# State-space mixer: order of the decay rows' loads, the sums of squares, the last output products and the norm

## The chip, the cores and the metric

The kernel runs on one core of a Trainium2 chip. A core has TensorE (matrix products; PE in the profile), VectorE (DVE), ScalarE (ACT), GpSimd (POOL) and SyncE (SP), which work beside one another, each through its own list of instructions in order, and wait for one another by semaphores. Data comes by DMAs that an engine's queue issues; here the weights come by SyncE's queue and the decay rows by ScalarE's. The metric is the device time of one launch in microseconds, the median of several runs.

## What is computed

A trunk of two layers over 512 tokens and 1024 features, in float32: an attention layer and a state-space layer, each followed by a convolutional feed-forward block and layer norms. The change lies in the second layer's mixer and the norm behind it, in the reference:

```python
def step(state, inp):                       # one chunk of 128 tokens
    xk, dtk, bk, ck = inp
    la = jnp.cumsum(dtk * a_g, axis=1)
    seg = la[:, :, None] - la[:, None, :]
    decay = jnp.exp(jnp.where(causal, seg, -jnp.inf))
    xdt = xk * dtk[..., None]
    cb = jnp.einsum('bign,bjgn->bijg', ck, bk)
    y = jnp.einsum('bijgh,bjghp->bighp', cb[..., None] * decay, xdt)
    y = y + jnp.einsum('bign,bghpn->bighp', ck, state) * jnp.exp(la)[..., None]
    ...                                     # state of the next chunk
y = y + d_skip[:, None] * xs
y = y.reshape(B, S, SSD_INNER) * jax.nn.silu(z)
y = group_rms_norm(y, norm_w)               # over the 512 features of a head group
return y @ w_out
...
x = layer_norm(DEEPNORM_ALPHA * x + m, ln_mix_g[i], ln_mix_b[i])
```

## The kernel before

Every large product is made in three passes (`mm3`, L105, L106, L107: high by high, high by low, low by high part of the operands). So each operand is split first: `split` copies the high part on ScalarE (L73) and subtracts it on VectorE (L76). Weights go through the same split, or, where a gain is folded in, through L98 and L99.

The mixer `ssd()` goes through four head groups g, and in each through four chunks c of 128 tokens. `Inputs(g).part(0..3)` makes a group's inputs: the projections and convolutions of B and C, of x, and of z (`acc<-xTh,w`, z on L1006 and L1007). While group g is scanned, the parts of group g+1 stand between its chunks and fill TensorE; so do the output products of group g-1 (`mixer_out`, `run_out`, `acc<-w,yT`), in the first two chunks. In the last group there are no further inputs.

`Scan.weights(c)` (L885) prepares the decays of a chunk: a DMA of 512 KB (L890, tile `lab`, also called E) puts the rows of the running sums into one of three buffers, TensorE makes cb (L893), ScalarE applies eight ReLUs (L897) and one exponential (L898), VectorE multiplies by cb (L899), GpSimd makes xdt (L901). `Scan.chunk(c)` (L911) loads el by two smaller DMAs (L922), makes the state product (L927), `intra` and `inter` (both L908), sums y on VectorE (L941 to L943), calls `weights(c + 1)`, multiplies by z (L948) and splits the result into `yT` (L73, L76). One yT tile holds two chunks. Then come the squares on ScalarE (L953), their sum over four blocks on VectorE (L955), the product `ss` with a column of ones on TensorE (L957) and the inverse root (L126 on VectorE, a power on GpSimd, L127), whose result `rsg` scales the output products where `run_out` adds them to the residual x (L861, VectorE).

After the last group `mixer_last` goes through the token tiles t = 0 to 3: output products of the group for both halves of the features, statistics (L179), then `Norm.finish`. Its ordinary form makes two passes on VectorE (L196, L197); its shared form, which the attention layer uses, scales on ScalarE (L192), multiplies on VectorE (L193) and adds on GpSimd (L194). `xT_of` then transposes x on TensorE (L136, tile `xTb`) and splits it for the feed-forward block.

The instructions are not in the order of the code: a scheduler places them on each engine by a planned timeline, within what buffers and operands allow. `acc` banks of PSUM are four, in two pairs; ss, cb, intra, inter and xTb take turns in four others.

## Time and profile before

| what | value |
|---|---|
| median of 3 runs | 1482.93 us (1482.7 to 1485.36) |
| profiled execution, time | 1487.44 us |
| its span | 1485.7 us, mean granted clock 0.992 |
| busy: TensorE, VectorE, ScalarE, GpSimd | 98%, 57%, 44%, 10% |

The span is what the profile covers of one execution; busy shares are of the span. The granted clock is that of TensorE, as a share of its full speed. A wait is idle time of an engine, put down to what ended last before it went on. The scan of the mixer reaches from about 745 to 1048 us, the norm behind it to about 1073.

### The profile page before, as it was taken

Reading aid. Unit: us, or ns where it says so; the run is one execution under the profiler, and the core shown is the slowest. Engines: PE = TensorE matmul, PEld = TensorE weight load, DVE = VectorE, ACT = ScalarE, POOL = GpSimd, SP = SyncE. Lnnn points to the kernel's source line nnn. Section 1 sums busy time; section 2 is a strip of 40 time slices with the busy share of each in tenths; the row PEclk is TensorE's granted clock in tenths of the full one; section 3 lists DMA queues with packets and bytes.
Section 4 is the critical chain, followed back from the end, with each engine's and each line's share of the span. In section 5 each row is a group of like instructions: output and inputs, shape, how many; then the busy total and the mean of one; then the engine's idle time right before and its main releaser. Section 6 shows DMA issues by size and latency. Waiting matters only on the chain.

```text
span 1485.7 us, 19157 instructions
## 1 busy us (share of the span) xinstructions
PE 1456.1 (98%) x7264; PEld 1199.8 (81%) x7264; DVE 851.5 (57%) x1465; ACT 658.7 (44%) x1261; POOL 142.1 (10%) x245
## 2 busy tenths in 40 slices
PE   9998999999999999999998999999799999999998
PEld 7875878888888888889876787887688888888887
DVE  5366786554545333846685867777854544433382
ACT  5476663443443222444765555453243443422331
POOL 2134313000000000000121101121100000000000
PEclk9999999999999999999999999999899999999999
DMA  6304142332333324423433332432232332333411
GB/s 232 110 29 153 58 146 72 100 98 88 99 99 100 99 86 164 139 69 117 118 121 100 107 122 90 128 118 95 87 100 99 93 98 93 100 100 93 162 57 57
DMA packets 51931, 155.92 MB, mean 105 GB/s; under 512 B 6400, under 2 KB 13312, under 8 KB 51840
## 3 DMA queue, kind: packets, MB, share of 16 engines
q1 hardware_dynamic: 39168, 135.49, 28.7%
q10 hardware_dynamic: 12672, 19.21, 4.1%
q8 instruction: 57, 0.93, 0.3%
q14 instruction: 34, 0.28, 0.1%
HBM read 148.26 MB, written 5.37 MB: 103 GB/s over the span
## 4 chain that ended last, share of the span: by engine, by line
PE 94%; DVE 3%; ACT 1%; DMA 1%; issue 1%; POOL 0%; ACTq 0%; DVEq 0%; POOLq 0%
PE acc L105 25%; PE acc L107 25%; PE acc L106 25%; PE pg L105 2%; PE pg L106 2%; PE pg L107 2%; PE s L329 1%; PE intra L908 1%; PE xTb L136 1%; PE pt L356 1%; PE o L368 1%; PE state L927 1%; PE inter L908 1%; DVE w L76 1%; PE om L105 1%
## 5 line engine op out<-in xcount | busy, mean ns | idle before, releaser
L76 DVE TENSOR_TENSOR w<-raw,w 128x512 fp32r<-128x512 f32 (+1 forms) x438 | 300.5, 695 | 288.5 <-ACT w L73 288.2
L73 ACT ACTIVATE w<-raw 128x512 fp32r<-128x512 f32 (+1 forms) x438 | 268.8, 625 | 422.5 <-PE acc L107 364.6
L106 PE MATMUL acc<-xTl,w 128*128 128x512 f32 (+1 forms) x1104 | 414.4, 376 | 0.5 <-DVE xTl L76 0.5
L105 PE MATMUL acc<-xTh,w 128*128 128x512 f32 (+1 forms) x1104 | 414.4, 377 | 0.0
L107 PE MATMUL acc<-xTh,w 128*128 128x512 f32 (+1 forms) x1104 | 414.0, 375 | 0.0
L106 PEld LDWEIGHTS acc<-xTl,w 128*128 128x128 f32 x1104 | 208.2, 189 | 37.8 <-issue 1.0
L107 PEld LDWEIGHTS acc<-xTh,w 128*128 128x128 f32 x1104 | 208.2, 189 | 37.6 <-issue 0.9
L105 PEld LDWEIGHTS acc<-xTh,w 128*128 128x128 f32 x1104 | 207.7, 189 | 37.7 <-DVE z L1007 0.5
L106 PE MATMUL acc<-w,h 128*128 128x512 f32 x352 | 137.1, 390 | 0.0
L107 PE MATMUL acc<-w,h 128*128 128x512 f32 x352 | 136.8, 390 | 0.0
L105 PE MATMUL acc<-w,h 128*128 128x512 f32 x352 | 136.7, 389 | 0.0
L604 DVE SCALAR_TENSOR_TENSOR conv<-acc,cw,conv 128x511 f32<-128x511 f32 x88 | 65.6, 746 | 87.7 <-ACT conv L602 87.7
L127 POOL TENSOR_TENSOR mv<-rs,half_neg 128x1 f32<-128x1 f32 x16 | 13.0, 815 | 754.8 <-DVE rs L126 754.8
L106 PEld LDWEIGHTS acc<-w,h 128*128 128x128 f32 x352 | 66.1, 188 | 13.7
L107 PEld LDWEIGHTS acc<-w,h 128*128 128x128 f32 x352 | 66.1, 188 | 13.6
L105 PEld LDWEIGHTS acc<-w,h 128*128 128x128 f32 x352 | 66.1, 188 | 13.6
L602 ACT ACTIVATE conv<-acc,cw 128x512 f32<-128x512 f32 x44 | 34.3, 780 | 84.1 <-PE acc L107 84.1
L628 DVE TENSOR_TENSOR conv<-conv,acc 128x512 f32<-128x512 f32 x44 | 30.2, 687 | 60.1 <-PE acc L107 57.6
L105 PE MATMUL acc<-w,yT 128*128 128x512 f32 x128 | 52.9, 413 | 3.8 <-ACT yT L73 3.8
L604 DVE SCALAR_TENSOR_TENSOR cv<-acc,scw,cv 128x511 f32<-128x511 f32 (+2 forms) x72 | 52.0, 740 | 6.0 <-ACT cv L602 5.7
L107 PE MATMUL acc<-w,yT 128*128 128x512 f32 x128 | 52.2, 410 | 0.6 <-DVE yT L76 0.6
L106 PE MATMUL acc<-w,yT 128*128 128x512 f32 x128 | 51.9, 405 | 0.0
(278 smaller groups left out, 2053.5 us busy)
## 6 DMA issues: line engine op xcount, KB each, us to landing
raw<-in_w_up SPq DMA_DIRECT2D x88, 512.0 KB, 3.5
raw<-in_w_down SPq DMA_DIRECT2D x44, 512.0 KB, 3.5
raw<-in_w_xbc SPq DMA_DIRECT2D x24, 512.0 KB, 3.6
raw<-in_w_ple_gate SPq DMA_DIRECT2D x16, 512.0 KB, 4.6
raw<-in_w_z SPq DMA_DIRECT2D x16, 512.0 KB, 3.5
lab<-rows ACTq DMA_DIRECT2D x16, 512.0 KB, 4.2
raw<-in_w_sout SPq DMA_DIRECT2D x16, 512.0 KB, 3.5
raw<-in_w_qkv SPq DMA_DIRECT2D x11, 512.0 KB, 4.6
```

The lines of the kernel that those rows point to most:

```text
L73: A.activation(h, src, AF.Copy)
L76: eng.tensor_tensor(l, src, h.bitcast(F32), op=OP.subtract)
L105: T.matmul(ps, lh, rh, start=start, stop=False)
L106: T.matmul(ps, lh, rl, start=False, stop=False)
L107: T.matmul(ps, ll, rh, start=False, stop=stop)
L136: T.transpose(b[:, k * P:(k + 1) * P], src[:, (half * 4 + k) * P:(half * 4 + k + 1) * P], ident)
L329: T.matmul(b[:, :e], q[:, ts], k[:, :e], start=n == 0, stop=n == len(qk) - 1)
L356: T.transpose(b[:, at:at + P], self.soft[x][2][i][:, t], ident)
L602: A.activation(f, ps, AF.Identity, bias=cw[:, taps:taps + 1], scale=cw[:, taps - 1:taps])
L604: V.scalar_tensor_tensor(f[:, k:], ps[:, :S - k], cw[:, taps - 1 - k:taps - k], f[:, k:], op0=OP.mult, op1=OP.add)
L628: V.tensor_tensor(g, g, pu, op=OP.mult)
L908: T.matmul(b[64 * x:64 * x + 64, k * P:(k + 1) * P], weights[:, h * 64:h * 64 + 64], moving(h), start=True, stop=True)
```

## The change

The decay rows and el of a chunk are fetched by a function of its own, `fetch(n)`, which `weights` calls for the following chunk, and which is called once for the first chunk ahead of all inputs. The sum over four blocks of squares is made by two additions in place of a reduction. The product ss and the inverse root leave `chunk` for `norm(c)`, which is called after the filling products of the chunk. In the last group, the output products of token tiles 0 and 1 are called within chunks 2 and 3 (`out_last`), ahead of these chunks' `norm`; those of tiles 2 and 3 stay behind the scan. And the norm behind the mixer takes its shared form.

```diff
-            def mixer_last(sc, w, ln, new, t):
-                for half in range(2):
-                    run_out(sc, w[half], half, t)
-                    ln.stats(t, xs[t], half)
-                ln.finish(t, xs[t], new)
+            ahead = {}
+
+            def fetch(n):
+
+                if n < 4 * NT:
+                    c = n % NT
+                    hs = slice(c * 32 + n // NT * 8, c * 32 + n // NT * 8 + 8)
+                    lab, el = three.tile([P, 8, P], F32, tag="lab", name="lab"), None
+                    nc.scalar.dma_start(lab.rearrange("p h i -> p (h i)"),
+                                        rows[hs, :].rearrange("h i -> (h i)").partition_broadcast(P))
+                    if c:
+                        el = two.tile([P, 4, P], F32, tag="el", name="el")
+                        for x in range(2):
+                            src = erows[hs, :].rearrange("(k x) i -> x k i", x=2)[x]
+                            nc.scalar.dma_start(el[64 * x:64 * x + 64], src.partition_broadcast(64))
+                    ahead[n] = lab, el

...
-                    E = three.tile([P, 8, P], F32, tag="lab", name="lab")
-                    nc.scalar.dma_start(E.rearrange("p h i -> p (h i)"),
-                                        rows[hs, :].rearrange("h i -> (h i)").partition_broadcast(P))
+                    E, el = ahead.pop(4 * g + c)
+                    fetch(4 * g + c + 1)
...
-                    self.E, self.xdt = E, xdt
+                    self.E, self.el, self.xdt = E, el, xdt
...
-                    E, xdt = self.E, self.xdt
+                    E, el, xdt = self.E, self.el, self.xdt
                     half, xd = c % 2, self.xd[c // 2]
                     hc = slice(half * P, (half + 1) * P)
-                    if c:
-                        el = two.tile([P, 4, P], F32, tag="el", name="el")
-                        for x in range(2):
-                            src = erows[hs, :].rearrange("(k x) i -> x k i", x=2)[x]
-                            nc.scalar.dma_start(el[64 * x:64 * x + 64], src.partition_broadcast(64))
...
                     sq = scr("sq").rearrange("p (k i) -> p k i", i=P)
                     A.activation(sq, y, AF.Square)
-                    s1 = st.tile([P, P], F32, tag="s1", name="s1", bufs=2)
-                    V.tensor_reduce(s1, sq.rearrange("p k i -> p i k"), axis=mybir.AxisListType.X, op=OP.add)
+                    V.tensor_tensor(sq[:, :2], sq[:, :2], sq[:, 2:], op=OP.add)
+                    self.sq = st.tile([P, P], F32, tag="s1", name="s1", bufs=2)
+                    V.tensor_tensor(self.sq, sq[:, 0], sq[:, 1], op=OP.add)
+
+                def norm(self, c):
                     b = bank("ss")
-                    T.matmul(b[:, :1], s1, ones[:, :1], start=True, stop=True)
+                    T.matmul(b[:, :1], self.sq, ones[:, :1], start=True, stop=True)

                     rsqrt(self.rs[:, c:c + 1], b[:, :1], 1.0 / 512, 4 * RMS_EPS)
...
+            fetch(0)
             ins = Inputs(0)
             for i in range(4):
                 ins.part(i)
             prev = None
+            last = {}
+
+            def out_last(half, t):
+                if t == 0:
+                    last[half] = load_out(3, half)
+                run_out(sc, last[half], half, t)
+
             for g in range(4):
                 sc = Scan(ins)
                 ins = Inputs(g + 1) if g < 3 else None
@@ -1020,12 +1036,19 @@
                         ins.part(c)
                     if prev and c < 2:
                         mixer_out(prev, c)
+                    elif not ins:
+                        for half in range(2):
+                            out_last(half, c - 2)
+                    sc.norm(c)
                 prev = sc
...
             ln = Norm(three, "ln_mix", 1, ("lab", "lab"))
             new = new_xT()
-            w = [load_out(3, half) for half in range(2)]
             for t in range(NT):
-                mixer_last(sc, w, ln, new, t)
+                for half in range(2):
+                    if t > 1:
+                        out_last(half, t)
+                    ln.stats(t, xs[t], half)
+                ln.finish(t, xs[t], new, True)
```

In the changed kernel the lines lie further down: the fetch's DMAs are L876 (lab) and L882 (el), ReLU and exponential L907 and L908, cb L903, the pairs of intra and inter L918, y L946 to L953, the squares L958, the two additions L959 and L961, ss L965, z L1014 and L1015.

ScalarE, end of group 0, where the decays of the next group's first chunk are prepared; raw and w are weights, y and z the tiles named above. Before:

```order
L890 DMA lab_7136<-rows_5715 128x1024
L922 DMA el_7342<-erows_5716 64x4x128
L897 ACTIVATE lab_7136<-lab_7136,la_5703 128x128 x8
L73 ACTIVATE w_7172<-raw_7170 128x512
L922 DMA el_7342<-erows_5716 64x4x128
L73 ACTIVATE yT_6584<-y_6699 128x4x128
L953 ACTIVATE sq_6724<-y_6699 128x512
L1006 ACTIVATE z_6733<-acc_6742 128x512
...
L73 ACTIVATE w_7175<-raw_7170 128x512
L898 ACTIVATE lab_7136<-lab_7136 128x1024
```

After:

```order
L876 DMA lab_6922<-rows_5715 128x1024
L73 ACTIVATE w_7184<-raw_7179 128x512
L907 ACTIVATE lab_6922<-lab_6922,la_5703 128x128 x8
L882 DMA el_6924<-erows_5716 64x4x128 x2
L908 ACTIVATE lab_6922<-lab_6922 128x1024
L73 ACTIVATE yT_6591<-y_6704 128x4x128
L958 ACTIVATE sq_6729<-y_6704 128x512
L1014 ACTIVATE z_6734<-acc_6743 128x512
```

The DMA stands where it stood, with the eight ReLUs behind it; a weight split is ahead of the ReLUs, and the exponential, which stood behind the z, is ahead of the split of y.

TensorE, last group, behind inter of chunk 2, from cb on: `yT_8547` is the tile of chunks 0 and 1. Before (31 products on that tile follow cb, the first 11 are shown):

```order
L893 MATMUL cb_8799<-CT_7685,BT_7684 128x128
L107 MATMUL acc_8919<-w_8892,yT_8547 128x512
L105 MATMUL acc_8919<-w_8897,yT_8547 128x512
L106 MATMUL acc_8919<-w_8897,yT_8547 128x512
L107 MATMUL acc_8919<-w_8897,yT_8547 128x512
L105 MATMUL acc_8919<-w_8900,yT_8547 128x512
L106 MATMUL acc_8919<-w_8900,yT_8547 128x512
L107 MATMUL acc_8919<-w_8900,yT_8547 128x512
L105 MATMUL acc_8959<-w_8873,yT_8547 128x512
L106 MATMUL acc_8959<-w_8873,yT_8547 128x512
L107 MATMUL acc_8959<-w_8873,yT_8547 128x512
L105 MATMUL acc_8959<-w_8876,yT_8547 128x512
```

After (`yT_8567` is that of chunks 0 and 1, `yT_8833` that of chunks 2 and 3):

```order
L903 MATMUL cb_8816<-CT_7695,BT_7694 128x128
L106 MATMUL acc_8950<-w_8876,yT_8567 128x512
L107 MATMUL acc_8950<-w_8876,yT_8567 128x512
L105 MATMUL acc_8950<-w_8881,yT_8567 128x512
L106 MATMUL acc_8950<-w_8881,yT_8567 128x512
L107 MATMUL acc_8950<-w_8881,yT_8567 128x512
L105 MATMUL acc_8950<-w_8884,yT_8567 128x512
L106 MATMUL acc_8950<-w_8884,yT_8567 128x512
L107 MATMUL acc_8950<-w_8884,yT_8567 128x512
L105 MATMUL acc_9037<-w_8843,yT_8833 128x512
L106 MATMUL acc_9037<-w_8843,yT_8833 128x512
```

Of the 31 products eight are left there; the others stand ahead of chunk 2's ss, and the ninth row behind cb reads chunk 2's yT.

TensorE, last group, at chunk 3, from ss to the first product that reads chunk 3's part of the yT tile (`acc_9071` before, `acc_9096` after). Before:

```order
L957 MATMUL ss_8823<-ones_5706,s1_8821 128x1
L908 MATMUL intra_8832<-lab_8797,xdt_8813 64x128 x8
L908 MATMUL inter_8841<-CT_7685,state_8772 64x128 x8
L107 MATMUL acc_9031<-w_8897,yT_8816 128x512
L105 MATMUL acc_9031<-w_8900,yT_8816 128x512
L106 MATMUL acc_9031<-w_8900,yT_8816 128x512
L107 MATMUL acc_9031<-w_8900,yT_8816 128x512
L105 MATMUL acc_9071<-w_8873,yT_8816 128x512
```

After:

```order
L965 MATMUL ss_8901<-ones_5706,s1_8839 128x1
L918 MATMUL intra_8907<-lab_8681,xdt_8830 64x128 x8
L918 MATMUL inter_8916<-CT_7695,state_8791 64x128 x8
L105 MATMUL acc_9096<-w_8843,yT_8833 128x512
L106 MATMUL acc_9096<-w_8843,yT_8833 128x512
L105 MATMUL acc_9112<-w_8873,yT_8833 128x512
```

The four products between inter and that first one are gone.

VectorE, from the last sums of squares' residuals to the first instruction of the norm that a transpose waits for. Before:

```order
L76 TENSOR_TENSOR w_9389<-raw_9387,w_9389 128x512
L861 SCALAR_TENSOR_TENSOR x_1547<-acc_9071,rsg_8492,x_1547 128x512
L861 SCALAR_TENSOR_TENSOR x_1547<-acc_9087,rsg_8492,x_1547 128x512
L76 TENSOR_TENSOR w_9392<-raw_9387,w_9392 128x512
L197 SCALAR_TENSOR_TENSOR x_1541<-lnt_8939,mv_8934,lnlab_8866 128x512
L197 SCALAR_TENSOR_TENSOR x_1541<-lnt_8949,mv_8934,lnlab_8866 128x512
```

After, where x is written by GpSimd behind L193:

```order
L76 TENSOR_TENSOR w_9198<-raw_9193,w_9198 128x512
L861 SCALAR_TENSOR_TENSOR x_1547<-acc_9096,rsg_8506,x_1547 128x512
L861 SCALAR_TENSOR_TENSOR x_1547<-acc_9112,rsg_8506,x_1547 128x512
L187 SCALAR_TENSOR_TENSOR mv_8978<-mv_8978 128x1
L76 TENSOR_TENSOR w_9417<-raw_9415,w_9417 128x512
L179 BN_STATS bn_9110<-x_1547 128x6
L187 SCALAR_TENSOR_TENSOR mv_9009<-mv_9009 128x1
L76 TENSOR_TENSOR w_9420<-raw_9415,w_9420 128x512
L187 SCALAR_TENSOR_TENSOR mv_9068<-mv_9068 128x1
L179 BN_STATS bn_9110<-x_1547 128x6
L193 TENSOR_TENSOR lnt_8984<-lnt_8984,lnlab_8969 128x512
L193 TENSOR_TENSOR lnt_8995<-lnt_8995,lnlab_8969 128x512
```

Where one weight split stood between the two residuals and the second pass, there are now one more split, two statistics and three small instructions (L187) ahead of the first multiplication.

## Rows read from the trace of the kernel before

**Rows 1.** The page's busy time by engine, and its chain by engine.
```profile
PE 1456.1 (98%) x7264; PEld 1199.8 (81%) x7264; DVE 851.5 (57%) x1465; ACT 658.7 (44%) x1261; POOL 142.1 (10%) x245
...
PE 94%; DVE 3%; ACT 1%; DMA 1%; issue 1%; POOL 0%; ACTq 0%; DVEq 0%; POOLq 0%
```

**Rows 2.** TensorE's waits, longest sums: us in total, times, longest.
```profile
PE ss L957 <- DVE s L955: 5.4, 1, 5.4
PE xTb L136 <- DVE x L197: 4.0, 1, 4.0
PE acc L105 <- ACT yT L73: 3.8, 1, 3.8
```

**Rows 3.** Stretches: us, busy PE PEld DVE ACT POOL, PEclk, DMA share, GB/s.
```profile
801.73:807.10 5.37, 0.00 (x1) 0.03 (x1) 2.38 (x4) 5.37 (x15) 0.00 (x0) 0.81 0.08 25
807.10:811.90 4.80, 4.80 (x11) 3.32 (x12) 4.24 (x8) 2.62 (x5) 2.30 (x2) 0.50 0.17 20
...
1047.37:1054.30 6.93, 6.30 (x14) 4.52 (x15) 5.77 (x10) 2.36 (x4) 0.00 (x0) 0.51 0.27 83
...
1061.10:1064.50 3.40, 3.39 (x15) 3.04 (x16) 3.40 (x6) 1.52 (x3) 0.00 (x0) 0.50 0.58 161
...
128.50:132.70 4.20, 2.62 (x15) 1.91 (x14) 4.20 (x9) 3.24 (x7) 1.53 (x2) 1.00 0.83 318
132.70:136.10 3.40, 3.40 (x12) 1.32 (x12) 2.12 (x4) 0.61 (x2) 3.27 (x9) 0.50 0.02 6
```

**Rows 4.** Timeline 795 to 811: start, us, engine, line, operation, [idle before, releaser].
```profile
795.97 0.32 ACTq L890 DMA_DIRECT2D lab<-rows  x1
...
801.73 0.40 ACT L897 ACTIVATE lab<-lab,la 128x128 f32<-128x128 f32 x1 [6.02 <-PE acc L107]
...
802.04 2.14 ACT L897 ACTIVATE lab<-lab,la 128x128 f32<-128x128 f32 x7
...
805.93 1.02 DVE L955 TENSOR_REDUCE s<-sq 128x128 f32<-128x512 f32 x1
...
808.07 1.05 ACT L898 ACTIVATE lab<-lab 128x1024 f32<-128x1024 f32 x1
...
809.01 1.42 PE L105 MATMUL acc<-xTh,w 128*128 128x512 f32 x1
```

**Rows 5.** Tile lab, 780 to 830: its DMAs from issue to landing.
```profile
DMA to landing us min/median/max: 3.6/4.2/5.7
```

**Rows 6.** Timeline 1028 to 1048, last group, columns as in rows 4.
```profile
1028.13 0.69 DVE L941 TENSOR_TENSOR y<-inter,el 128x512 f32<-128x512 f32 x1 [1.15 <-PE inter L908]
...
1028.58 0.39 PE L105 MATMUL acc<-w,yT 128*128 128x512 f32 x1
...
1032.65 0.63 ACT L73 ACTIVATE yT<-y 128x512 fp32r<-128x512 f32 x1 [10.85 <-DVE y L948]
...
1033.96 0.39 PE L107 MATMUL acc<-w,yT 128*128 128x512 f32 x1
...
1041.41 1.04 PE L908 MATMUL inter<-CT,state 128*64 128x128 f32 x16
...
1047.37 0.75 PE L105 MATMUL acc<-w,yT 128*128 128x512 f32 x1 [3.79 <-ACT yT L73]
```

**Rows 7.** Timeline 1060 to 1073 and 1012, and the instructions of line 194.
```profile
1060.31 1.40 DVE L197 SCALAR_TENSOR_TENSOR x<-lnt,mv,lnlab 128x512 f32<-128x512 f32 x2
...
1061.11 3.72 PE L136 MATMUL xTb<-cst,x 128*128 128x128 f32 x16 [4.00 <-DVE x L197]
...
1068.82 0.99 POOL L127 TENSOR_TENSOR mv<-rs,half_neg 128x1 f32<-128x1 f32 x1 [8.90 <-DVE rs L126]
...
1072.56 0.36 PE L106 MATMUL acc<-xTl,w 128*128 128x256 f32 x1
...
1012.70 1.04 POOL L901 TENSOR_TENSOR xdt<-xf,dt 128x512 f32<-128x512 f32 x1
...
L194 POOL TENSOR_TENSOR x<-lnt,lnc x8: 1277/1519/1787, 237.2 to 258.7; 128x512 f32<-128x512 f32 x8
```

## Prediction

> **What bounds the kernel now.** I read the page's busy shares and its chain first: TensorE is busy 98% of a span of 1485.7 us and carries 94% of the chain that ended last [rows 1]. So an edit pays or costs only where it changes what TensorE waits for, or the clock at which it works behind a wait. I then read TensorE's own list of waits. Its three longest lie in the state-space mixer and its norm, and they are the three places that the change touches [rows 2]: 5.4 us for the sums of squares (place A, end of head group 0), 3.8 us for yT (place B, last group) and 4.0 us for the first transposes after the norm (place C). Third comes a table of stretches, for the granted clock behind such waits [rows 3]. Behind each of the three the clock is at its lower level (0.50 or 0.51, 1.2 GHz of 2.4): 4.80 us at A, 6.93 us at B, 3.40 us at C. Half of such a stretch is lost, 2.4, 3.5 and 1.7 us. A short break can also be followed by it: in a stretch of 4.20 us TensorE was busy 2.62 us, and the next 3.40 us ran at 0.50. During the wait at A the mean clock was 0.81, so (1 - 0.81) / 0.5 x 5.37 = 2.0 us of the slow stretch had passed before work came back: a longer wait swallows more of it. All the rest is read for these places alone.
>
> **Decay rows one chunk ahead (place A).** The wait at A is put down to the sums of squares, but these are only last in a queue. The DMA of decay rows is issued at 795.97, when intra has released one of three buffers; it lands late, and ScalarE stands before the first ReLU until 801.73 [rows 4]. Behind the eight ReLUs come the split of y, the squares and the four z, and behind those VectorE's reduction and TensorE's ss at 807.10. The fetch is written a chunk earlier now, but the order of ScalarE shows the DMA in its old place: behind the same activations, waiting for the same release, with the eight ReLUs one instruction behind it. So the early fetch earns 0 here. Three things do change. Ten more products stand before intra; a 512-column product steps by (1033.96 - 1028.58) / 23 = 0.234 us [rows 6], so the release comes 2.3 us later, at about 798.3. Landings near there took 3.6 to 5.7 us, median 4.2 [rows 5], where this one took 5.7: ReLUs would start at 801.9 to 804.0, with the median at 802.5. And the exponential, 1.05 us, stands ahead of the split, the squares and the z, where it stood behind them [rows 4]. ss itself has gone behind the filling products, but the next of these needs a PSUM bank that z holds. From the first ReLU to the first free bank I count 2.4 (ReLUs), 1.0, three steps of 0.5 and VectorE's z of some 0.7, some 5.6 to 6.0 us, against 5.37 before. TensorE is then back at 807.9 to 810.0, at the median 808.5, with ss, cb and state still to do (807.10 to 809.01 before). Against 809.01 that is +0.8 to +1.4 at the median and +2.9 at the late end. Take +1.0, with -0.8 (early landing, and the clock back sooner because the wait is longer) to +2.4. The same DMA in the other chunks is covered by 50 and more products, as before.
>
> **Reduction as two adds, ss behind the products.** One reduction of about 1.0 us per chunk becomes an add of 256 columns and one of 128 on VectorE, perhaps 0.55 us together by the 0.69 us of a 512-column one [rows 6]; sixteen times some 0.45 us, 7 us of VectorE. VectorE has 57% of the span [rows 1], and except at A no product waits for this reduction. At A it no longer stands before the first z, which the 5.6 us above already contain. 0 beyond that, and if the cover were gone not over 0.5 us a chunk.
>
> **Output products inside the last chunks (place B).** Before, 31 products stand between cb of chunk 2 and the first that needs chunk 2's yT; from the step on y that inter releases (1028.13) to the split yT (1032.65 + 0.63 = 1033.28) it takes 5.2 us [rows 6], and 31 x 0.234 = 7.3 us cover it. Now the products of the first two token tiles have run earlier, and only 8 are left there: 8 x 0.234 and 0.24 for cb cover 2.1 us. VectorE's queue in between has the same y steps and one residual, as before. So a wait appears that the trace of before doesn't have: 5.2 - 2.1 = **+3.1 us**. At chunk 3 the four products that stood behind inter are gone. There the first product on yT came 1047.37 - 1042.45 = 4.9 us after the end of inter (1041.41 + 1.04) [rows 6]; with no filling at all, and one residual more in VectorE's queue ahead, the wait is about 5.0 us instead of 3.8, **+1.2 us**. What clock follows the new wait has no row of its own: nothing at the least, 3.5 us at the most (as behind the 3.8 us wait), and 1.7 us behind the break of 1.6 us [rows 3]. I take +1.7, since 3.1 us lies between the two and the work ahead of it is dense. Behind the later wait 24 products follow, as many as before; 1.2 us more of the slow stretch is swallowed by the wait, -0.6 (0 to -1.0, where as much as at A is swallowed).
>
> **Norm on three engines (place C).** Before, VectorE does both passes. TensorE waits from 1057.1 to 1061.11 for the first transposes, and the product behind the last ones starts at 1072.56 [rows 7]. Now ScalarE scales, VectorE multiplies and GpSimd adds, and each transpose waits for GpSimd. The same three-engine form ran in layer 0 of this trace: GpSimd's add took 1.28 to 1.79 us, median 1.52, while a GpSimd operation of that size took 1.04 in a quiet stretch [rows 7]. Before, one weight split lay between the two last residuals and the second pass at 1060.31; in the new order two splits and two statistics do, three instructions of some 0.65 us more, so the first multiply ends at about 1062.9 and the first add at 1064.5: TensorE idles some 7.4 us where it idled 4.0. Then the adds run one after another on GpSimd, eight in all with one power of 0.99 us among them: 8 x 1.52 + 0.99 = 13.2, the last done at 1062.9 + 13.2 = 1076.1, the transposes more than a microsecond later, at 1077.5. By then 9 more products of 256 columns are done, by half of 0.234 us each 1.1 us. 1077.5 - 1072.56 - 1.1 = **+3.8 us**. With GpSimd at 1.04 the late start alone is left, +0.9; with 1.79, +5.9. In layer 0 other products covered this norm; here nothing is left to fill with. I take 1.52, because VectorE is as busy beside it here. The Trainium skill ("SBUF - State Buffer", Who interferes with whom) calls the SBUF port pair that VectorE shares with GpSimd an exclusive lock; the spread of layer 0's adds above the quiet 1.04 agrees, and by that rule the larger price is the one that holds.
>
> **Sum.** +1.0 (A) + 3.1 + 1.2 + 1.7 - 0.6 (B) + 3.8 (C) = +10.2 us. Against the profiled span that is 1495.9, against the profiled run's 1487.44 us 1497.6. That run is 4.5 us over the median of the runs, a difference that both kernels should have; on the scale of the median the forecast is 1482.9 + 10.2 = **1493.1 us**.
>
> **Rivals.**
> First, the fetch does what it says: the landing comes before ScalarE needs it. Then the wait at A and its slow stretch go, -5.4 - 2.4 = -7.8 us instead of +1.0, and the total is +1.4, 1484.3 us, not slower by what can be told. It decides if the ReLUs start within 3.5 us of intra's end at A. Against it: the DMA is released by the same buffer, and no landing there was under 3.6 us. Chance 0.08.
> Second, VectorE is what bounds place C. Between the last sums of squares and the last transposes it now does eight second passes and three first ones of 0.70 us (1.40 for two) [rows 7], and it would do eight multiplies of 0.69: 11 x 0.70 - 8 x 0.69 = 2.2 us less. If GpSimd keeps pace, C gives -2.2 instead of +3.8, total +4.2, 1487.1 us. It decides if the adds take about 1.0 us and the wait before the first transpose is no longer than 4 us. The Trainium skill ("Perfetto Trace Analysis", Optimizing Scalar/DVE Operations) says that with a saturated VectorE moving work to ScalarE or even GpSimd may make sense, and warns of the shared port; the windows at C show VectorE busy 3.40 of 3.40 us [rows 3]. Against it: 1.28 us is the shortest add in layer 0. Chance 0.13.
> Third, the waits swallow the slow clock: no fall behind the new wait (0 instead of 1.7), none behind the later one (-4.1 instead of -0.6), and the 1.7 us of C's slow stretch lie in its longer wait. Total 10.2 - 1.7 - 3.5 - 1.7 = +3.3, 1486.2 us. For it: 2.0 us were swallowed so at A. Against it: the slow stretch at B began only with the work. Chance 0.12.
> Fourth, everything goes late: a landing of 5.7 us at A (+2.4), a full slow stretch behind the new wait (+3.5), adds of 1.79 (+5.9): +2.4 + 3.1 + 1.2 + 3.5 - 0.6 + 5.9 = +15.5, 1498.4 us. Chance 0.07.
>
> **How the numbers follow.** The forecast's own case has 0.60; its terms' ends, not all at once, reach from about 1488 to 1497. Two of the first three rivals together would end at 1477 to 1480, faster; this is small and I give it and its like 0.08. A single one of them ends near or a little over the bound of 0.2% (3 us, about what a measurement of this kernel can tell from no change), with some spread on both sides: 0.15 within it. The rest, 0.77, is slower. The range 1483.5 to 1497.5 takes in all single rivals but the fourth, and leaves out some 0.15.
>
> **What would show it.** In the changed trace: TensorE's list of waits with five entries over 2.5 us from this mixer instead of three; at A the first ReLU no earlier than 3.6 us after the issue, and a wait of 6 us or more put down to z; at B a new wait of about 3 us for the yT of chunk 2 and one of about 5 us for chunk 3's; at C a wait of about 7 us before the first transposes, for GpSimd, and adds of about 1.5 us. The forecast is wrong if the adds take 1.0 us, if the ReLUs of A start early, or if the products before chunk 2's yT cover it.

## The result, and the profile after

| kernel | median of the runs | profiled execution: time, span |
|---|---|---|
| before | 1483.2 us (1482.7 to 1485.36) | 1487.44 us, 1485.7 us |
| changed | 1495.93 us (1494.44 to 1497.78) | 1497.78 us, 1495.5 us |

The changed kernel takes 1.0084 times as long as the one before, with a 95% interval of 1.0066 to 1.0101: 9.8 to 15.0 us more, at the middle 12.5. The forecast was 1493.1 us, +9.9 on the median of before in this table, in a range of 1483.5 to 1497.5.

The page of the changed kernel, busy time and chain by engine, beside [rows 1]:

```profile
PE 1455.9 (97%) x7264; PEld 1200.3 (80%) x7264; DVE 847.3 (57%) x1477; ACT 665.1 (44%) x1269; POOL 152.8 (10%) x253
...
PE 93%; DVE 3%; POOL 1%; ACT 1%; issue 1%; DMA 1%; ACTq 0%; DVEq 0%; POOLq 0%
```

TensorE's work is the same (1455.9 us, 1456.1 before). The span has grown by 9.8 us at equal busy time, so the loss is waiting: at half clock a 512-column product is listed with 0.63 us instead of 0.39, so a slow clock would have shown as busy time. TensorE's three longest waits, which answer to [rows 2] (total, times, longest):

```profile
PE xTb L136 <- POOL x L194: 9.5, 4, 7.8
PE acc L105 <- ACT yT L73: 7.9, 2, 4.9
PE acc L105 <- DVE z L1015: 7.0, 1, 7.0
```

In this order they are places C, B and A, and they answer to 4.0, 3.8 and 5.4 us before. Each of the three has grown, and B has a second wait. The stretches behind and in them, as [rows 3]: length, busy PE, PEld, DVE, ACT, POOL, granted clock of TensorE, DMA share, GB/s.

```profile
800.95:807.93 6.98, 0.01 (x3) 0.01 (x1) 4.87 (x9) 5.80 (x14) 0.00 (x0) 0.75 0.42 130
807.93:811.10 3.17, 3.17 (x8) 2.50 (x9) 1.93 (x4) 0.69 (x2) 0.00 (x0) 0.50 0.00 0
...
1036.47:1039.42 2.95, 0.00 (x0) 0.00 (x0) 2.92 (x6) 0.68 (x2) 0.00 (x0) 1.00 0.01 4
1039.42:1043.20 3.78, 3.78 (x10) 2.98 (x11) 1.32 (x4) 0.47 (x1) 0.00 (x0) 0.57 0.00 0
...
1053.77:1057.00 3.23, 3.23 (x8) 2.55 (x9) 1.33 (x4) 1.10 (x2) 0.00 (x0) 0.50 0.56 176
...
1061.30:1069.09 7.79, 0.00 (x2) 0.00 (x1) 7.35 (x15) 4.80 (x8) 4.62 (x6) 0.66 0.64 217
1069.09:1077.40 8.31, 6.63 (x28) 5.43 (x29) 7.30 (x9) 3.49 (x6) 7.95 (x6) 0.50 0.01 2
```

At A TensorE is idle for 6.98 us, with the clock already down for a part of it (0.75), and works at half clock for 3.17 us. At B the new wait of 2.95 us is followed by 3.78 us at 0.57, and the later one by only 3.23 us at 0.50, where it was 6.93 us. At C the wait is 7.79 us, and behind it come 8.31 us at half clock in which TensorE is busy for 6.63.

**Where the time went.** TensorE has done the same work at the end of the last output product and at the first 512-column product of the feed-forward block. Between the first `bk` of the mixer (706.43 before, 706.00 now) and the last output product (1057.1 and 1061.3) the trace gained 355.3 - 350.7 = 4.6 us: places A and B. From there to the 512-column product (1091.36 and 1100.91) it gained 39.6 - 34.3 = 5.35 us: place C. The attention layer gave 0.4 back and the rest lost 0.3: in all 9.8.

Place A, first the timeline of the changed kernel (start, us, engine, operation, idle before), as [rows 4]:

```profile
796.57 1.09 PE L918 MATMUL intra<-lab,xdt 128*64 128x128 f32 x16
...
797.71 0.32 ACTq L876 DMA_DIRECT2D lab<-rows  x1
...
802.10 0.40 ACT L907 ACTIVATE lab<-lab,la 128x128 f32<-128x128 f32 x1 [1.50 <-DMA lab<-rows]
...
804.58 1.06 ACT L908 ACTIVATE lab<-lab 128x1024 f32<-128x1024 f32 x1
...
807.93 0.80 PE L105 MATMUL acc<-xTh,w 128*128 128x512 f32 x1 [6.97 <-DVE z L1015]
```

The DMA of decay rows is issued at 797.71, right behind intra, which ended at 797.66 (796.57 + 1.09), although the code fetches it a chunk earlier. The first ReLU starts at 802.10, with the exponential ahead of the z, and TensorE is back 5.83 us later.

One sentence ahead of the prediction was wrong: the tile of that DMA, `lab_7136` before and `lab_6922` now, belongs not to the first but to the third chunk of the next group. It is the seventh of the sixteen and takes the buffer of the fourth, so both kernels fetched two to three chunks ahead.

Place C, the norm in the changed kernel, beside [rows 7]:

```profile
1066.04 1.88 DVE L193 TENSOR_TENSOR lnt<-lnt,lnlab 128x512 f32<-128x512 f32 x3
...
1066.79 8.50 POOL L194 TENSOR_TENSOR x<-lnt,lnlab 128x512 f32<-128x512 f32 x5 [3.17 <-DVE lnt L193]
...
1067.95 3.31 DVE L193 TENSOR_TENSOR lnt<-lnt,lnlab 128x512 f32<-128x512 f32 x2
...
1069.09 1.11 PE L136 MATMUL xTb<-cst,x 128*128 128x128 f32 x4 [7.79 <-POOL x L194]
1070.76 1.12 PE L136 MATMUL xTb<-cst,x 128*128 128x128 f32 x4 [0.56 <-POOL x L194]
```

And its instructions by line: count, duration in ns (min/median/max), first and last start.

```profile
L193 DVE TENSOR_TENSOR lnt<-lnt,lnlab x8: 673/692/1751, 1066.0 to 1078.6; 128x512 f32<-128x512 f32 x8
...
L194 POOL TENSOR_TENSOR x<-lnt,lnlab x8: 1268/1708/2246, 1066.8 to 1080.4; 128x512 f32<-128x512 f32 x8
```

GpSimd's additions take 1.27 to 2.25 us, median 1.71. Two of VectorE's multiplications take 3.31 us together, where three took 1.88. The transposes come in groups of four at the pace of GpSimd, 1.67 us apart.

### The profile page after: what moved, and what is told of

It reads as the page before. It is cut to its first block, busy times and chain, and to the rows that moved or that the text cites. A ratio compares the mean times of both kernels' runs of the same rounds, so it can differ in the third digit from the quotient of the medians.

```text
span 1495.5 us, 19187 instructions
## 1 busy us (share of the span) xinstructions
PE 1455.9 (97%) x7264; PEld 1200.3 (80%) x7264; DVE 847.3 (57%) x1477; ACT 665.1 (44%) x1269; POOL 152.8 (10%) x253
## 3 DMA queue, kind: packets, MB, share of 16 engines
HBM read 148.26 MB, written 5.37 MB: 103 GB/s over the span
## 4 chain that ended last, share of the span: by engine, by line
PE 93%; DVE 3%; POOL 1%; ACT 1%; issue 1%; DMA 1%; ACTq 0%; DVEq 0%; POOLq 0%
PE acc L105 25%; PE acc L106 24%; PE acc L107 24%; PE pg L107 2%; PE pg L105 2%; PE pg L106 2%; PE s L329 1%; PE xTb L136 1%; PE intra L918 1%; PE pt L356 1%; PE o L368 1%; PE state L932 1%; DVE w L76 1%; PE inter L918 1%; PE om L105 1%
## 5 line engine op out<-in xcount | busy, mean ns | idle before, releaser
L602 ACT ACTIVATE conv<-acc,cw 128x512 f32<-128x512 f32 x44 | 34.3, 780 | 84.3 <-PE acc L107 84.3
L105 PE MATMUL acc<-w,yT 128*128 128x512 f32 x128 | 52.9, 415 | 7.9 <-ACT yT L73 7.9
L106 PE MATMUL acc<-w,yT 128*128 128x512 f32 x128 | 52.2, 408 | 0.0
L907 ACT ACTIVATE lab<-lab,la 128x128 f32<-128x128 f32 x128 | 39.6, 389 | 27.5 <-DMA lab<-rows 27.5
```

What stands on the lines that cost most here:

```text
L105: T.matmul(ps, lh, rh, start=start, stop=False)
L106: T.matmul(ps, lh, rl, start=False, stop=False)
L602: A.activation(f, ps, AF.Identity, bias=cw[:, taps:taps + 1], scale=cw[:, taps - 1:taps])
L907: A.activation(E[:, h], E[:, h], AF.Relu, bias=la[:, hs][:, h:h + 1], scale=-1.0)
```

## The experiments

Ratios are to the kernel before on the same chip; the difference is the ratio's excess on 1484 us. A trace is one execution. The trace of before seems to be a long one: in all thirteen kernels of the table the timed difference lies 0.6 to 3.4 us above what a trace shows against it from the first `bk` to the 512-column product. So kernels are compared by their timed ratios, and traces are read for where a wait stands.

| run | ratio (95%) | difference | waits A; B; C, longest (us) |
|---|---|---|---|
| changed | 1.0084 (1.0066 to 1.0101) | +12.5 | 7.0; 2.9 and 4.9; 7.8 |
| e1 norm in its ordinary form | 1.0053 (1.0038 to 1.0068) | +7.9 | 7.4; 2.9 and 4.9; 4.5 |
| e2 B's order as before | 1.0068 (1.0053 to 1.0083) | +10.1 | 7.4; 4.3; 8.1 |
| e3 no early fetch | 1.0081 (1.0066 to 1.0097) | +12.0 | 7.2; 2.9 and 4.9; 7.8 |
| e4 three-engine norm alone | 1.0045 (1.0028 to 1.0062) | +6.7 | 5.0; 3.8; 8.2 |
| e5 addition on VectorE | 1.0070 (1.0055 to 1.0085) | +10.4 | 7.1; 2.9 and 4.9; 7.9 |
| e6 fourth buffer, SyncE's queue | 1.0021 (1.0011 to 1.0031) | +3.1 | 3.5; 3.8; 4.9 |
| e7 squares alone | 1.0025 (1.0015 to 1.0036) | +3.7 | 7.1; 4.3; 5.4 |
| e8 changed, norm early | 1.0037 (1.0023 to 1.0052) | +5.5 | 7.6; 2.9 and 5.4; 0.9 |
| e9 before, norm early | 1.0018 (1.0009 to 1.0028) | +2.7 | 4.1; 2.0 and 3.6; 4.1 |
| e10 e9 with additions | 1.0032 (1.0021 to 1.0043) | +4.7 | 6.7; 3.1 and 3.6; 4.1 |
| e11 fourth buffer, GpSimd's queue | 1.0054 (1.0039 to 1.0069) | +8.0 | 6.6; 3.8; 4.5 |
| e12 one fetch less | 0.9985 (0.9976 to 0.9994) | -2.2 | 2.0; 3.8; 4.3 |

**e1, the norm.**

```diff
-                ln.finish(t, xs[t], new, True)
+                ln.finish(t, xs[t], new)
```

> The changed kernel with the norm behind the mixer in its ordinary form again (both passes on VectorE); all else as changed. Theory (the sum by places, with place C at +5.6 us as the changed trace shows it): 1495.9 - 5.6, about 1490 us; the wait before the first transposes goes from 7.8 to about 4 us, the waits at A (7.0) and B (2.9 and 4.9) stay. Rival (VectorE bounds the norm, the three-engine form relieves it and the loss lies at B): no faster than 1496 us.

Measured 1492.11 us, ratio 1.0053. By the middles of the two ratios the norm's form is worth 0.0031, 4.6 us, near the 5.6 expected, though the ends of their intervals overlap (1.0066 to 1.0068). It is e4 below that shows this price clear of the noise. TensorE's waits in this kernel stand as foretold:

```profile
PE acc L105 <- ACT yT L73: 7.9, 2, 4.9
PE acc L105 <- DVE z L1015: 7.4, 1, 7.4
PE xTb L136 <- DVE x L197: 4.5, 1, 4.5
```

**e2, place B.** The kernel before, with the additions, ss behind the filling products and the three-engine norm. Without the early fetch and the calls in the last chunks the scheduler puts 31 products behind inter of chunk 2 again.

```diff
...
-                    T.matmul(b[:, :1], s1, ones[:, :1], start=True, stop=True)
+                    self.s1 = s1
+
+                def norm(self, c):
+                    b = bank("ss")
+                    T.matmul(b[:, :1], self.s1, ones[:, :1], start=True, stop=True)
...
-                ln.finish(t, xs[t], new)
+                ln.finish(t, xs[t], new, True)
```

> The kernel before with the two additions, ss behind the filling products and the three-engine norm, without the early fetch and without the output products called inside the last chunks; in this combination 31 products stand behind inter of chunk 2 again, where the changed kernel has 8. Theory (place B at +3.5): 1495.9 - 3.5, about 1492.4 us, no wait for yT of chunk 2, about 4.5 us for that of chunk 3, A and C as in the changed kernel. Rival (B costs nothing, since the slow clock falls into its waits): about 1496 us.

Measured 1495.36 us, ratio 1.0068: 2.4 us under the changed kernel, of 3.5 expected, with overlapping intervals: the times do not rule out the rival, that B costs nothing. What is shown is the wait, for that on chunk 2's yT is gone:

```profile
PE xTb L136 <- POOL x L194: 10.4, 4, 8.1
PE acc L105 <- DVE z L1011: 7.4, 1, 7.4
PE acc L105 <- ACT yT L73: 4.3, 1, 4.3
```

In the two traces the mixer is 3.4 us shorter than in the changed kernel, as foretold, and the norm 2.9 us longer. Here the transposes come eight by eight, with a wait of 1.2 us between the two groups and one of 1.4 us behind them, as they do in e4, where C's price is larger than in the changed kernel too. So part of what B gives back may be paid at C.

**e3, the fetch.**

```diff
...
-                    ahead[n] = lab, el
+                    return lab, el
...
-                    E, el = ahead.pop(4 * g + c)
-                    fetch(4 * g + c + 1)
+                    E, el = fetch(4 * g + c)
...
-            fetch(0)
```

> The changed kernel with the decay rows and el loaded by weights of the same chunk again; all else as changed. Theory (the early fetch moves no DMA): within 1.5 us of the changed kernel, 1496 us, with the wait at A still about 7 us and B unchanged. Rival (the fetch earns something that the other edits hide): slower than the changed kernel by 3 us or more, with waits of ScalarE for the decay rows longer in several chunks.

Measured 1496.85 us, ratio 1.0081 against 1.0084. The early fetch is worth nothing that can be told.

**e4, the norm alone.**

```diff
-                ln.finish(t, xs[t], new)
+                ln.finish(t, xs[t], new, True)
```

> The kernel before with only the norm behind the mixer in its three-engine form. Theory (C adds up with the others): 1483.2 + 5.6, about 1489 us, with a wait of about 8 us before the first transposes and additions of GpSimd of 1.3 to 2.2 us. Rival (C's loss needs the products that B has moved ahead): about 1483 to 1485 us.

Measured 1491.45 us, ratio 1.0045, +6.7 us (4.2 to 9.2). The norm costs at least as much without the rest of the change.

```profile
PE xTb L136 <- POOL x L194: 10.5, 4, 8.2
PE ss L957 <- DVE s L955: 5.0, 1, 5.0
PE acc L105 <- ACT yT L73: 3.8, 1, 3.8
```

A and B stand as before, and C alone has doubled.

**e5, who makes the norm slow.** The changed kernel with the last of the three steps on VectorE, in this norm only (`l_` is set there).

```diff
-                    G.tensor_tensor(y[:, s], tmp, self.b[:, s], op=OP.add)
+                    (V if l_ else G).tensor_tensor(y[:, s], tmp, self.b[:, s], op=OP.add)
...
```

> The changed kernel with one edit: in the norm behind the mixer GpSimd's addition is made by VectorE, so that GpSimd does no work of 512 columns there; ScalarE's scaling and VectorE's multiplication stay. Theory (the norm's price is GpSimd's 1.7 us per addition and what it does to VectorE beside it): VectorE's multiplications back at about 0.7 us each, none of the 1.0 to 1.8 us of the changed trace, the wait before the first transposes shorter by 1 to 1.5 us, the total 3 to 5 us under the changed kernel, 1491 to 1493 us. Rival (the late start behind ScalarE and VectorE's queue is the whole price, and two passes of 16 instructions fill VectorE): no faster than 1495 us.

Measured 1494.76 us, ratio 1.0070, 2.1 us under the changed kernel with overlapping intervals. Durations of the two steps here (min/median/max in ns), against 1268/1708/2246 for GpSimd's addition above:

```profile
L193 DVE TENSOR_TENSOR lnt<-lnt,lnlab x8: 637/682/685, 1065.2 to 1075.6; 128x512 f32<-128x512 f32 x8
L194 DVE TENSOR_TENSOR x<-lnt,lnlab x8: 679/682/684, 1067.6 to 1078.0; 128x512 f32<-128x512 f32 x8
```

Without GpSimd beside it no multiplication takes over 0.69 us: the long ones of the changed kernel came from GpSimd's additions. But the wait before the first transposes is 7.9 us still, which the theory had put 1 to 1.5 us shorter, and the time is close to the 1495 us that the rival names. So the long wait needs no addition on GpSimd; it fits the late start. By times e5 lies midway, 2.1 us under the changed kernel and 2.5 us above e1, with intervals that overlap on both sides, so what GpSimd's additions cost in time is not shown.

**e6, the landing at A.** The kernel before, with a fourth buffer and another queue; a scratch pool has three buffers instead of five to make room.

```diff
-    sp = pool("sp", 5)
+    sp = pool("sp", 3)
...
+            labs = lpool("labs", 4)
...
-                    E = three.tile([P, 8, P], F32, tag="lab", name="lab")
-                    nc.scalar.dma_start(E.rearrange("p h i -> p (h i)"),
+                    E = labs.tile([P, 8, P], F32, tag="lab", name="lab")
+                    nc.sync.dma_start(E.rearrange("p h i -> p (h i)"),
```

> The kernel before with a fourth buffer for the decay rows, whose DMA goes by SyncE's queue instead of ScalarE's; a scratch pool has three buffers instead of five to make room. So the DMA for place A waits neither for intra of the chunk just computed nor for ScalarE's activations. Theory (the wait at A is the landing of this DMA, and with it go 5.0 to 5.4 us of waiting and 2.4 us of slow clock): the wait for the sums of squares at A is gone or under 1 us, total 5 to 8 us under the kernel before, 1476 to 1479 us. Rival (the squares and z behind it are late for another reason): a wait at A of 3 us or more stays, total within 2 us of before.

Measured 1487.65 us, ratio 1.0021: slower, a miss. The fourth buffer did not take the wait away. Place A in this kernel:

```profile
799.22 1.09 PE L909 MATMUL intra<-lab,xdt 128*64 128x128 f32 x16
...
800.35 0.33 SPq L891 DMA_DIRECT2D lab<-rows  x1
...
803.78 2.45 ACT L898 ACTIVATE lab<-lab,la 128x128 f32<-128x128 f32 x8 [0.51 <-DMA lab<-rows]
```

Its DMA was issued at 800.35, when intra (799.22 to 800.31) had released a buffer. With four buffers the scheduler fetches one tile more, the eighth instead of the seventh, and its ReLUs stand at the same place, ahead of yT. TensorE came back at 808.56, 4.8 us after the first ReLU. That is the same chain without the weight split. So this run didn't test the landing. It also changed C, where the wait is 4.9 us and a second one of 1.7 us follows; whether that comes from the smaller scratch pool was not run.

**e7, additions and ss alone.** The kernel before, with the two additions and ss moved as in e2.

> The kernel before with the two additions and with ss behind the filling products, and nothing else of the change: place A alone, with B's order and the norm as before. Theory (A at +0.8 to +1.2 us): 1484 to 1485 us, a wait of about 7 us for z at A instead of 5.4 for the sums of squares, waits at B and C as before. Rival (two additions free VectorE and ss no longer blocks): 1480 us or less.

Measured 1488.18 us, ratio 1.0025, +3.7 us (2.2 to 5.3), above the 1 us expected. The wait at A is as foretold, but the others are not as before:

```profile
PE acc L105 <- DVE z L1011: 7.1, 1, 7.1
PE xTb L136 <- DVE x L197: 5.4, 1, 5.4
PE acc L105 <- ACT yT L73: 4.3, 1, 4.3
```

C has 5.4 us where it had 4.0, and B 4.3 for 3.8. The same small edits have changed the order at the end of the last group too: behind inter of chunk 3 two products are left of four, and 2 x 0.234 = 0.47 us is what B's wait has gained; at C one more weight split stands on VectorE ahead of the inverse root, and all 24 products stand ahead of the last ss, where 23 did.

**e8, an early norm.** The changed kernel with the ordinary norm, where tiles 0 and 1 get statistics and norm right behind their output products.

```diff
...
                     elif not ins:
+                        if c == 2:
+                            ln = Norm(three, "ln_mix", 1, ("lab", "lab"))
+                            new = new_xT()
                         for half in range(2):
                             out_last(half, c - 2)
+                            ln.stats(c - 2, xs[c - 2], half)
+                        ln.finish(c - 2, xs[c - 2], new)
...
```

> The changed kernel, but in the last group statistics and norm of token tiles 0 and 1 are written right behind their output products, inside chunks 2 and 3, and the norm has its ordinary form; so their transposes and some 40 products of the feed-forward block stand ahead of the transposes of tiles 2 and 3. Theory (the wait at C is the late start of a norm that stands behind the last sums of squares): the wait before the transposes is under 2 us, the slow stretch behind it gone or short, 5 to 9 us under e1_norm_plain, which differs by the place of the norm alone: 1483 to 1487 us, with the waits at A and B as in the changed kernel. Rival (TensorE then waits for the splits of x instead): 1490 us or more.

Measured 1489.77 us, ratio 1.0037. TensorE around the transposes:

```profile
1065.28 1.03 PE L136 MATMUL xTb<-cst,x 128*128 128x128 f32 x8
1066.15 0.28 PE L965 MATMUL ss<-ones,s 128*128 128x1 f32 x2
1067.35 0.50 PE L105 MATMUL acc<-xTh,w 128*128 128x256 f32 x2 [0.92 <-ACT xTh L73]
```

The transposes of tile 1 stand ahead of the last ss, and no wait over 0.92 us is left at C; the clock there is 1.00. Against e1 that is 2.4 us, with overlapping intervals, of 5 to 9 expected. The norm lies beside chunk 3 now, whose yT comes later (5.4 us instead of 4.9), and behind that wait this trace has 7.1 us at half clock, where that of the changed kernel has 3.23 and that of e1 6.07:

```profile
1055.88:1062.97 7.09, 6.57 (x15) 4.68 (x16) 6.14 (x11) 2.36 (x4) 0.00 (x0) 0.50 0.28 84
```

So nothing was won on the clock at B. That a late norm makes the wait at C is shown; that an early one pays in full is not.

**e9 and e10, an early norm on the kernel before,** with output products and norm of tiles 0 and 1 inside the last chunks as in e8, without and with the additions in place of the reduction:

```diff
-                    V.tensor_reduce(s1, sq.rearrange("p k i -> p i k"), axis=mybir.AxisListType.X, op=OP.add)
+                    V.tensor_tensor(sq[:, :2], sq[:, :2], sq[:, 2:], op=OP.add)
+                    V.tensor_tensor(s1, sq[:, 0], sq[:, 1], op=OP.add)
```

> The kernel before, with the output products and the norm of tiles 0 and 1 written inside the last two chunks, and nothing else of the change: 31 products stand behind inter of chunk 2, as before. Theory: the 4.0 us wait at C and its slow clock (1.7 us) go, and the transposes ahead of chunk 3 change little at B: 4 to 7 us under the kernel before, 1477 to 1480 us. Rival: the norm's VectorE work delays y of chunk 3, and B grows by as much as C shrinks: 1483 us.

> As e9, with the two additions in place of the reduction. Theory (the additions are worth nothing off place A, where the reduction stands before ss): within 2 us of e9. Rival: VectorE's shorter work shows at B and C, and it is 3 us or more under e9.

Measured 1487.21 us (1.0018) and 1489.51 us (1.0032). Neither gains: e9 misses the 4 to 7 us that it was to win. In e9 the transposes of tile 0 are placed ahead of chunk 3's intra and wait for the norm, and those of tile 1 still come behind the last ss:

```profile
PE xTb L136 <- DVE x L197: 6.2, 2, 4.1
PE ss L957 <- DVE s L955: 4.1, 1, 4.1
PE acc L105 <- ACT yT L73: 3.6, 1, 3.6
```

So the 4 us wait stays and a new one of 2.0 us stands before it. e10 lies 2.0 us above e9, at the bound of what was to count as nothing; its wait at A has gone over to z with 6.7 us, so the two additions alone turn the order at A.

**e11, the landing once more.** The kernel of e6, with GpSimd's queue in place of SyncE's; the cut is against the kernel before.

```diff
-                    nc.scalar.dma_start(E.rearrange("p h i -> p (h i)"),
+                    nc.gpsimd.dma_start(E.rearrange("p h i -> p (h i)"),
```

> The kernel before with a fourth buffer for the decay rows and their DMA issued by GpSimd's queue, where no weight loads stand ahead of it (in e6_fourth_buffer it stood behind those of SyncE and came at 800.4 us). Theory (the wait at A is the late landing): the rows land well before 800 us, the wait at A is under 1 us, 5 to 8 us under the kernel before. Rival (the squares, z and splits are late for another reason): 3 us or more of waiting stay at A.

Measured 1492.28 us, ratio 1.0054, a miss like e6: the DMA was issued at 797.78, again one tile further ahead, the first ReLU came at 803.69 and TensorE at 808.46. Here TensorE also waits 3.0 us for z at 718.0, early in the mixer, where e6 waits 0.8 us and the other kernels not at all; the cause is open, and its +8.0 us are not the price of A alone.

**e12, the wait's cause taken away.** The kernel before without the load at A; GpSimd fills its tile with zeros instead.

```diff
+                    if g == 1 and c == 2:
+                        G.memset(E, 0.0)
+                    else:
+                        nc.scalar.dma_start(E.rearrange("p h i -> p (h i)"),
+                                            rows[hs, :].rearrange("h i -> (h i)").partition_broadcast(P))
```

> The kernel before, with one of the 16 loads of decay rows left out: the one at place A, whose tile (chunk 2 of group 1) is filled with zeros by GpSimd as soon as intra has released it; that chunk's decays are thus not computed from the inputs. Theory (the landing of this DMA sets the first ReLU, and TensorE comes back 5.4 to 5.8 us after that): the first ReLU within 2 us of the release, the wait at A 1 to 2 us instead of 5.4, the slow clock behind it gone, 4 to 6.5 us under the kernel before. Rival (y, squares and z are late by themselves): a wait of 4 us or more stays at A, total within 1.5 us of before.

Measured 1480.8 us, ratio 0.9985. GpSimd fills the tile from 795.47 on, ScalarE's ReLUs start at 796.46, and TensorE waits 2.0 us; the exponential stands ahead of the split of y here. The two instructions, then the stretches of this wait and behind it:

```profile
795.47 0.95 POOL L891 MEMSET lab<- 128x1024 f32 x1
...
796.46 1.28 ACT L900 ACTIVATE lab<-lab,la 128x128 f32<-128x128 f32 x4 [1.77 <-POOL lab L891]
...
800.71:802.71 2.00, 0.00 (x0) 0.03 (x1) 1.78 (x3) 2.00 (x5) 0.00 (x0) 1.00 0.00 0
802.71:810.00 7.29, 7.29 (x32) 5.79 (x33) 5.89 (x9) 2.62 (x6) 3.01 (x3) 1.00 0.24 74
```

The cause of A's wait is settled: with the landing gone it falls from 5.4 to 2.0 us, and the clock behind it stays at 1.00. The size is a miss: the time falls by 2.2 us (0.9 to 3.6), against 4 to 6.5 expected. In the traces 5.5 us are gone between `bk` and the 512-column product, against one long execution of before; which of the two is nearer to A's whole price stays open. It is no version to use, since a chunk's decays are missing. None of the versions that compute everything beats the kernel before.

## Why the prediction was right

**The fetch moves nothing: right,** by e3. Why: the scheduler had already issued each load as soon as a buffer came free, and a load's place is set by that release. e6 and e11 show that more buffers only move the same meeting one tile on.

**A: right at its own place; what its edits did elsewhere was left out.** Foretold were the first ReLU at 802.5 and TensorE back at 808.5, measured 802.10 and 807.93. The first ReLU came 4.4 us after intra's end, so the first rival, which wanted 3.5 or less, is out. Over five kernels TensorE comes back at a distance from the first ReLU that the order between them sets: 5.37 us before (801.73 to 807.10) and 5.38 in e9 (796.67 to 802.05), 5.83 in the changed kernel and 5.82 in e7 (799.26 to 805.08), where the exponential stands ahead, and 4.8 in e6. e12 took away the landing, and 3.4 of the 5.4 us went. At the place itself the changed trace gained 1.6 us of wait and lost 1.6 us of half-clock work behind it (3.17 for 4.80), half of which counts: +0.8, near the +1.0 forecast. But the edits of A alone cost 3.7 us in e7, not 1.0. The step that failed is "0 beyond that" for the additions and the moved ss: they reordered the end of the last group as well, where the waits at B and C grew by 0.5 and 1.4 us. I had counted that end only for all the edits together.

**B's waits: right; its clock: one term mis-sized, one right by luck.** The new wait was 2.95 us (forecast 3.1), the later one 4.92 (5.0), the slow clock behind the new one 0.43 x 3.78 = 1.6 us (1.7). The last 24 products, put at -0.6, took 1061.30 - 1053.77 = 7.5 us instead of 9.7 [rows 3]: -2.2. Only 3.23 us of half clock fell on the work, but not because the longer wait had swallowed the rest, as the prediction's term and the third rival have it: over that wait the clock was 0.98, so the slow stretch itself was shorter here than before. So B's sum is +3.5 in the trace, not +5.4; by times, as far as e2 tells, 2.4. That 1.6 met the 1.7 is luck. In e1 TensorE has the same products around this wait, and it too waits 2.95 us, but the stretch behind it is at full clock:

```profile
1038.99:1042.80 3.81, 3.81 (x16) 3.12 (x17) 1.32 (x4) 0.47 (x1) 0.00 (x0) 1.00 0.00 0
```

In e8, behind the same 2.95 us, 7.88 us follow at 0.57. So one trace gives no price for the clock behind a wait. B's cause was named too narrowly: output products called inside the last chunks need not move the products, for e9 has them, with an early norm, and lacks the second wait on yT; nor do the additions and the moved ss, by e7 and e2. Together they do, with or without the fetch (e3) and with either form of the norm (e1).

**C: right in kind and too small.** The wait was 7.79 us (forecast 7.4). The additions were longer than the 1.52 us taken from layer 0, with a median of 1.71, and VectorE's multiplications beside them up to 1.75. And the sum had no term for a longer slow stretch at C: the clock stayed at 0.50 for 8.31 us (3.40 before), while transposes came in groups. 5.35 us in the trace, 4.6 (e1) to 6.7 (e4) by times, against 3.8. By e5 the late start stays when GpSimd is out; how the time divides between it and the additions stays open. The low end that the prediction gives this term, +0.9 with additions of 1.04 us, does not come out of its own chain: eight additions shorter by 0.48 us take off 3.8, and about 0 is left. The second rival, that VectorE's relief would win, is refuted by e4.

**The sum.** A's edits +3.7 (e7), B +2.4 (changed less e2) and C +6.7 (e4) make 12.8, against 12.5 measured and 10.2 forecast (1.0, 5.4 and 3.8). Two terms were too small and one too large, so that the total came near is in part luck. The errors of the single ones go from 1.6 us (e7) over 2.5 (e4) to some 3 for a difference of two ratios. And B is itself what the changed kernel has over e2, so the sum tests one thing alone: that A's edits and C's add up in e2, 3.7 + 6.7 = 10.4 against 10.1 measured.

**The signs.** The prediction wanted five waits over 2.5 us from this mixer. Its own terms make four (one at A, two at B, one at C), and four are there.

**From the trace to the median: wrong.** I took the 4.5 us between the profiled run and the median as common to both kernels. The changed kernel's profiled run lies 1.9 us over its median, so spans differ by 9.8 us and medians by 12.7. The profiled run of before was a long one of its kind: all timed runs of that kernel here lie between 1482.07 and 1487.2 us.

## What to carry to other kernels

Where a scheduler places instructions, read the order of the changed kernel before crediting an edit: an early call moved no DMA here, and two short additions with a moved product changed waits at the other end of the scan. A norm shared by three engines has a longer chain, and at a joint with nothing to fill that chain is the price (e4); whether it pays where products fill its time, as in layer 0, no run here tests. And what stands behind a late load's first reader in an in-order queue waits with it, so look at who follows the reader, not only at who needs the data.

## What the runs showed of the hardware

VectorE and GpSimd lengthen each other when both read two operands from SBUF: VectorE's multiplication of 128x512 took 0.68 us alone (e5) and up to 1.75 us beside GpSimd's additions, and these took 1.27 to 2.25 us where GpSimd's products in a quiet stretch took 1.04 [rows 7]. The Trainium skill ("SBUF - State Buffer", Who interferes with whom) says that a VectorE instruction with two SBUF inputs contends with a GpSimd instruction that reads SBUF, and calls the port pair that they share an exclusive lock. The pace of about 1.7 us for both agrees, since 0.68 and 1.04 us one after the other make 1.72.

The slow clock can begin inside a wait: the mean over the 6.97 us wait at A was 0.75, and over the 7.79 us at C 0.66. And a longer wait need not be followed by more slow work: behind 3.79 us came 6.93 us at 0.51 [rows 3], behind 4.92 us 3.23 us at 0.50. Nor is the same wait followed by the same: behind 3.79 us e4 has 3.56 us at 0.52, and behind 2.95 us the clock was 1.00 in e1 and 0.57 for 3.78 us in the changed kernel. Behind the 2.0 us wait of e12 there was no slow stretch at all, but behind a wait of 2.04 us in e9 the next 4.66 us had a mean of 0.63, and the table of before has a slow stretch behind a break of 1.6 us [rows 3]:

```profile
1044.19:1047.75 3.56, 3.56 (x9) 2.79 (x10) 2.10 (x3) 1.10 (x2) 0.00 (x0) 0.52 0.55 167
1039.34:1044.00 4.66, 4.66 (x40) 4.04 (x40) 2.97 (x6) 1.20 (x2) 0.00 (x0) 0.63 0.00 0
```

(The first line is e4, the second e9.) What decides it in each case stays open here.
